# A decoder layer on one core: the first modulation and projection in quarters, with weights laid out in 4 KB pieces

## The chip, the cores and the metric

The kernel runs on one core of one Trainium2 chip. TensorE is called PE here (its weight loads PEld), VectorE DVE, ScalarE ACT, GpSimd POOL, and SyncE SP, which issues most DMAs. The metric is device time in microseconds (us) of one execution.

## The reference, cut to what matters

```python
mod = silu(c) @ w_ada + b_ada                  # (1, 6144); only the first 2048 columns matter here
shift1, scale1, ... = split(mod, 6)
h = rms_norm(x, norm1_g) * (1 + scale1) + shift1   # x: 1024 tokens x 1024
proj = h @ w_in                                # 1472 columns
q_lat, kv_lat, k_rope, x_lru, g_lru = split(proj)
# then attention on q_lat, kv_lat, k_rope; a gated linear recurrence on x_lru, g_lru;
# output projection, residual, and a routed expert FFN with the other four parts of mod
```

## The kernel before, in words

The tokens are taken in two halves of 512 (`n` or `hf` is 0 or 1). For each half, `stats(hf)` squares and sums the four 128-token tiles of x (`sq`, on ACT and DVE), takes the inverse root by a chain of small DVE operations (`rsq`, tiles `rs_x`, `rs_t`, result `iv8`) and scales the tiles in place. `turn(hf)` transposes them on PE into eight tiles `pt`, of which two PSUM banks hold two at a time. `modulate(hb)` computes half of shift1 and scale1: 32 products of a broadcast `silu(c)` with tiles `wada` into `pm`, then a copy `mrow0`, a turn into columns, and two small DVE operations that give `modc` and `sc1`. `lift(k)` applies them to the k-th slice (ACT, `xT`) and splits it into a rounded part `hTh` (a cast on DVE) and a rest `hTl` (a subtraction on DVE, for every fourth k on POOL).

The projection runs over twelve tiles of `w_in` (table `FT`: 0 `kl`, 1 `ql`, 2 `xl`, 3 `ql`, then three `xl`, `kr` and four `gl`). `load_in(i)` fetches tile i, `split_in(i)` splits it into `winh` (ACT) and `winl` (POOL for the first three, DVE after). `project(i, n)` is three matmuls of 128x512 for each of eight k, 24 in all, into a bank `pp`, of which there are three; `evac(i, n)` empties it: for tile 0 `latkh` (ACT), `latkl` (DVE) and squares `sqq`, for tile 1 `latq` and `sqq`, for an `xl` tile `xr` and `xc` (ACT), then three DVE operations for the convolution and a split `xch`, `xcl`. `sqq` goes to PE in matmuls `pc` with one column.

Before the change three tiles (K1 = 3) of half 0 are projected while `modulate(1)` is still being computed; `stats(1)` is written behind them, then the second half of the same three tiles, slice by slice with `turn(1)`; the other tiles follow, each with n = 0 and n = 1. From there on the recurrence's gates (`pg` matmuls, DVE chain from `lq` to a scan) are woven in, and the rest of the modulation (`wad`, `ada`). `rotary()` computes tables of sines and cosines on DVE and ACT (`rb`, `tab`); a short DVE chain (`ld`, `lp`) prepares the recurrence's constants. Each engine executes its list in order; the order comes from a scheduler that places the written instructions by its own estimates, except that SP keeps the written order through this stage (`pin`), and `issue_after` holds an instruction behind another. SP keeps up to eight transfers in flight.

Of the kernel before, what the change touches and what calls it, by code (L numbers as in the profile page):

```python
# [1774 lines left out]
```

## Time and profile before

| | |
|---|---|
| median of 3 runs | 814.96 us (814.83 to 815.29) |
| the profiled execution's own time | 816.14 us |
| its span (first to last instruction) | 814.4 us |
| PE busy in the span | 730.2 us (90%) |
| first matmul of the projection | 29.96 us after the span's start |
| three tiles, half 0 done | 56.6 us |
| three tiles, half 1 done | 78.9 us |

Read it like this: the profiled execution is one of its own, 1.2 us above the median, and 1.7 us of its time lie outside the span. The stage that the change touches ends at about 80 us; the other 730 us follow from it in order.

### The profile page before, as it was taken

To read this page: it belongs to the slowest core of one execution; us is meant where nothing else is said; L and a number is where in the kernel's file an instruction comes from. 1 tells how busy PE (TensorE), PEld (TensorE's weight loads), DVE (VectorE), ACT (ScalarE), POOL (GpSimd) and SP (SyncE) were. 2 spreads that over 40 slices of the span, in tenths; PEclk is the share of its full clock that TensorE was granted. 3 is DMA by queue.
4 is the path that set the end of the run, shared out by engine and by line. 5 is a ranking of instruction groups with operands and counts; after the bars stand their busy time and mean duration, and the time that the engine had idled before them with its cause. 6 is when DMAs were issued, how large, how long until landed. Compare 5 with 4: busy or idle time off the path is not lost. (4 is left out here: it accounts for less than half of the span.)

```text
span 814.4 us, 12262 instructions
## 1 busy us (share of the span) xinstructions
PE 730.2 (90%) x4257; PEld 470.3 (58%) x4257; DVE 447.6 (55%) x1334; ACT 317.3 (39%) x715; POOL 157.6 (19%) x150
## 2 busy tenths in 40 slices
PE   3799999989988989899999997699988789999994
PEld 1377776548876878788888886333233234333231
DVE  4597386869776468788884667434333122221311
ACT  3455456675344156667664444221201112120210
POOL 1121012102766102031311000212112111221101
PEclk9999999999999999999999998799989999999999
DMA  9952437682307403020154699899999999999993
GB/s 312 374 149 85 143 118 236 211 269 84 119 9 281 156 27 104 1 79 1 60 193 140 237 340 345 329 294 344 335 345 319 358 369 331 336 365 341 349 313 64
DMA packets 70976, 180.47 MB, mean 222 GB/s; under 512 B 8960, under 2 KB 22528, under 8 KB 70912
## 3 DMA queue, kind: packets, MB, share of 16 engines
q1 hardware_dynamic: 63328, 158.50, 54.9%
q0 software_dynamic: 7104, 21.00, 9.7%
q8 instruction: 34, 0.56, 0.3%
q10 hardware_dynamic: 480, 0.16, 0.1%
q14 instruction: 30, 0.25, 0.1%
HBM read 160.61 MB, written 22.95 MB: 225 GB/s over the span
## 5 line engine op out<-in xcount | busy, mean ns | idle before, releaser
L1649 PE MATMUL pgu<-ew,xeT 128*32 128x512 f32 (+1 forms) x928 | 166.4, 620 | 7.7 <-DMA ew<-in_w_e 7.5
L1649 PEld LDWEIGHTS pgu<-ew,xeT 128*32 128x32 f32 (+1 forms) x928 | 47.8, 122 | 100.2 <-issue 82.2
L1660 PE MATMUL py<-ew,hT 128*32 128x512 f32 (+1 forms) x464 | 78.5, 596 | 4.4 <-ACT hT L1634 4.4
L225 PE MATMUL pp<-hTh,winh 128*128 128x512 f32 x176 | 68.2, 400 | 5.8 <-DVE hTh L188 3.0
L226 PE MATMUL pp<-hTl,winh 128*128 128x512 f32 x176 | 70.1, 398 | 0.2 <-DVE hTl L469 0.2
L227 PE MATMUL pp<-hTh,winl 128*128 128x512 f32 x176 | 69.5, 396 | 0.0
L1663 DVE TENSOR_TENSOR y<-py,m_g 128x512 f32<-128x512 f32 (+1 forms) x40 | 27.6, 691 | 74.9 <-PE py L1660 70.0
L1623 ACT ACTIVATE sg<-pgu 128x256 f32<-128x256 f32 (+1 forms) x20 | 7.7, 386 | 130.4 <-PE pgu L1649 130.4
L1660 PEld LDWEIGHTS py<-ew,hT 128*32 128x32 f32 (+1 forms) x464 | 23.9, 120 | 49.8 <-issue 38.5
L1616 DVE TENSOR_SCALAR xeT<-pxe,gc,mc 128x128 f32<-128x128 f32 x80 | 27.4, 403 | 38.2 <-PE pxe L1610 38.2
L1634 ACT ACTIVATE hT<-pht 128x256 f32<-128x256 f32 (+1 forms) x20 | 7.6, 381 | 98.0 <-PE pht L1632 86.1
L1665 POOL DMA_INDIRECT out<-y,pki x13 | 20.7, 1594 | 115.4 <-DVE y L1663 91.3
L225 PEld LDWEIGHTS pp<-hTh,winh 128*128 128x128 f32 x176 | 33.4, 190 | 16.2 <-DVE hTh L188 4.0
L1625 DVE SCALAR_TENSOR_TENSOR hid<-sg,pkw,pgu 128x256 f32<-128x256 f32 (+1 forms) x13 | 6.2, 477 | 63.5 <-ACT sg L1623 63.5
L1614 ACT ACTIVATE xeT<-pxe,mc,gc 128x128 f32<-128x128 f32 x80 | 30.0, 461 | 25.9 <-PE pxe L1610 25.9
L226 PEld LDWEIGHTS pp<-hTl,winh 128*128 128x128 f32 x176 | 33.4, 190 | 9.9 <-issue 2.1
L227 PEld LDWEIGHTS pp<-hTh,winl 128*128 128x128 f32 x176 | 33.4, 190 | 8.3 <-DVE lq L587 0.8
L949 ACT ACTIVATE P<-pS,nb,scq 128x384 f32<-128x384 f32 (+2 forms) x48 | 32.3, 679 | 12.2 <-DVE nb L946 12.2
L983 PE MATMUL po<-PT,v 128*128 128x256 f32 (+1 forms) x160 | 35.8, 362 | 0.0
L1046 POOL TENSOR_TENSOR wo<-wo,m_g 128x256 f32<-128x256 f32 x32 | 28.2, 917 | 15.5 <-DMA wo<-in_w_out 15.5
L1610 PEld LDWEIGHTS pxe<-ident,xe 128*128 128x128 f32 x160 | 18.4, 145 | 21.0 <-issue 15.7
L983 PEld LDWEIGHTS po<-PT,v 128*128 128x128 f32 x160 | 28.8, 191 | 2.9
(424 smaller groups left out, 1615.0 us busy)
## 6 DMA issues: line engine op xcount, KB each, us to landing
ew<-in_w_e SPq DMA_DIRECT2D x186, 512.0 KB, 7.2
wad<-in_w_ada SPq DMA_DIRECT2D x64, 256.0 KB, 4.0
wada<-in_w_ada SPq DMA_DIRECT2D x16, 512.0 KB, 10.8
win<-in_w_in SPq DMA_DIRECT2D x12, 512.0 KB, 7.5
xt<-in_x SPq DMA_DIRECT2D x8, 512.0 KB, 6.6
wo<-in_w_out SPq DMA_DIRECT2D x8, 512.0 KB, 6.1
xr<-in_x SPq DMA_DIRECT2D x8, 512.0 KB, 4.6
x_d<-xr SPq DMA_DIRECT2D x8, 512.0 KB, 2.7
```

The costliest lines, as they stand in the source:

```text
L225: T.matmul(o, lhi, rhi, start=first, stop=False)
L226: T.matmul(o, lhi, rlo, start=False, stop=False)
L227: T.matmul(o, llo, rhi, start=False, stop=last)
L949: SC.activation(Pt[:, o:o + w], pss[ci], AF.Exp, scale=P["scq"][:, i:i + 1], bias=nb, accum_out=l[:, ci:ci + 1])
L983: T.matmul(po[:, o:], P["v"][:, js], PT[j // 4][:, j % 4, o:], start=(j == 0), stop=(j == nj - 1), skip_group_check=True)
L1046: EN[OPT["g1"]].tensor_mul(w[:, q:q + 256], w[:, q:q + 256], mrow["g1"][:, q:q + 256])
L1614: SC.activation(xT[a][:, c], pt[:, c], AF.Identity, scale=gc[:, k:k + 1], bias=sh2[:, k:k + 1])
L1616: last["dve"] = V.tensor_scalar(xT[a][:, c], pt[:, c], gc[:, k:k + 1], sh2[:, k:k + 1], op0=OP.mult, op1=OP.add).ins
L1649: T.matmul(pg[r], xT[k // 4][:, c + r.start:c + r.stop], w[k // 2][:, NS[k % 2]], start=(k == 0), stop=(k == 7), skip_group_check=True)
L1660: T.matmul(py[n][r], hT[:, a * 128 + r.start:a * 128 + r.stop], w[4 + a][:, NS[n]], start=(a == 0), stop=(a == 1), skip_group_check=True)
L1663: last["dve"] = V.tensor_mul(y[:rows, NS[n]], py[n][:rows], mrow["g2"][:rows, NS[n]]).ins
L1665: G.indirect_dma_start(out=out, out_offset=bass.IndirectOffsetOnAxis(ap=idx, axis=0), in_=y[r0:r0 + idx.shape[0]], in_offset=None, compute ...
```

## The change

`modulate` is called for quarters (two slices k each, 32 products of 128 columns) in place of halves (four slices, 256 columns); its copy `mrow0` moves from ACT to DVE. The loads of `w_in` tiles 0 to 2 stand between those of the modulation's quarters, then tile 3, the second half of x and tile 4. After each quarter its two slices are lifted, the next `w_in` tile is split, and the tiles that are there advance by these slices. Tile 3 is projected for n = 0 behind `stats(1)`, so that its second visit does n = 1 alone. Every `winl` and `hTl` is now computed on DVE. `rotary()` no longer starts at the head and is drained later; the chain `ld`, `lp` is held behind the scaling of the last x tile. On the host, `w_in` is laid out as one contiguous 4 KB row for each partition and tile (before: eight pieces of 512 B), and the first 2048 columns of `w_ada` as rows of 4 KB (before: pieces of 2 KB).

```diff
@@ -114,7 +114,7 @@
...
-... "lo": "VVVG", ... "in_l1": "G", ...
+... "lo": "VVVV", ... "in_l1": "V", ...
@@ -247,12 +247,9 @@
         kind, j = FT[i]
-        M = 64 if kind == "kr" else 128
-        f0 = FCOL[kind] + j * 128
-        w = blk("win")
-        v = t3(w, 8)[:, :, :M]
-        SY.dma_start(v, A["w_in"][:, f0:f0 + M].rearrange("(k p) f -> p k f", p=128))
-        wraw[i] = v
+        w = blk("win")[:, :512 if kind == "kr" else 1024]
+        SY.dma_start(w, A["w_in"][i * 128:(i + 1) * 128, :w.shape[1]])
+        wraw[i] = t3(w, 8)
 
@@ -279,22 +276,22 @@
     load_x(0)
-    for i in range(OPT["lw"]):
-        load_in(i)
     wada = {}
 
-    def load_ada(hb):
-        for k in range(8):
-            w = wada[hb, k] = blk("wada")
-            SY.dma_start(t3(w, 2), A["w_ada"][k * 128:(k + 1) * 128, :2048].rearrange(
-                "p (s h d) -> p s h d", s=2, h=2)[:, :, hb])
-
-    load_ada(0)
-    for i in range(OPT["lw"], OPT["lw2"]):
-        load_in(i)
-    load_ada(1)
-    for i in range(OPT["lw2"], OPT["lw4"]):
-        load_in(i)
+    def load_ada(q):
+        for k in range(4):
+            w = blk("wada")
+            r = (q * 4 + k) * 128
+            SY.dma_start(w, A["w_ad0"][r:r + 128, :])
+            wada[q, 2 * k], wada[q, 2 * k + 1] = w[:, :512], w[:, 512:]
+
+    for q in range(4):
+        if q < 3:
+            load_in(q)
+        load_ada(q)
+    load_in(3)
+    load_x(1)
+    load_in(4)
     row = const.tile([128, NROW], F32, name="row")
@@ -365,7 +362,7 @@
             if OPT["xsc"][t] == "V":
-                V.tensor_scalar(xs[t], xs[t], iv8[:, t:t + 1], None, op0=OP.mult)
+                last["xsc"] = V.tensor_scalar(xs[t], xs[t], iv8[:, t:t + 1], None, op0=OP.mult).ins
             else:
@@ -382,8 +379,7 @@
     stats(0)
-    for i in range(OPT["lw"]):
-        split_in(i)
+    split_in(0)
     drain(turn(0))
@@ -437,26 +433,21 @@
 
-    def modulate(hb):
-        pm = bank("pm")[:, :256]
+    def modulate(q):
+        pm = bank("pm")[:, :128]
         for k in range(8):
-            yield
             for i in range(4):
-                T.matmul(pm[32 * i:32 * i + 32], cs32[:, k, :], wada[hb, k][:, i * 256:i * 256 + 256],
+                T.matmul(pm[32 * i:32 * i + 32], cs32[:, k, :], wada[q, k][:, i * 128:i * 128 + 128],
                          start=(k == 0), stop=(k == 7), skip_group_check=True)
-        mrow0 = half("mrow0")[:, :256]
-        SC.activation(mrow0, pm, AF.Copy)
+        mrow0 = half("mrow0")[:, :128]
+        V.tensor_copy(mrow0, pm)
         pm2 = bank("pm2")
-        for c in range(2):
-            T.matmul(pm2[:, c:8:2], mrow0[:, c * 128:(c + 1) * 128], ident[:, 0:128:32], start=True, stop=True)
-        hs = slice(hb * 4, hb * 4 + 4)
-        V.tensor_add(t3(modc, 2)[:, :, hs], t3(pm2[:, :8], 2), t3(C("bada"), 2)[:, :, hs])
-        V.scalar_tensor_tensor(sc1[:, hs], modc[:, 8 + hb * 4:12 + hb * 4], 1.0, C("n1g")[:, hs], op0=OP.add, op1=OP.mult)
+        T.matmul(pm2[:, :4], mrow0, ident[:, 0:128:32], start=True, stop=True)
+        hs = slice(q * 2, q * 2 + 2)
+        V.tensor_add(t3(modc, 2)[:, :, hs], t3(pm2[:, :4], 2), t3(C("bada"), 2)[:, :, hs])
+        V.scalar_tensor_tensor(sc1[:, hs], modc[:, 8 + q * 2:10 + q * 2], 1.0, C("n1g")[:, hs], op0=OP.add, op1=OP.mult)
 
     rot = rotary()
-    if OPT["ro"] == 0:
-        next(rot)
-    drain(modulate(0))
     sh1 = modc[:, 0:8]
@@ -467,14 +458,6 @@
         EN[OPT["lo"][k % 4]].tensor_sub(hTl[k][:, ns], xT[k], hTh[k][:, ns])
-
-    for k in range(4):
-        lift(k, xT[k], 0)
-    for i in range(OPT["lw4"], OPT["lw3"]):
-        load_in(i)
-    load_x(1)
-    for i in range(OPT["lw3"], OPT["k1"]):
-        load_in(i)
 
@@ -677,26 +660,21 @@
     K1 = OPT["k1"]
-    mod = modulate(1)
-    split_in(1)
-    if OPT["ro"] == 1:
-        next(rot)
-    for i in range(K1):
-        for k in range(4):
-            drain(project(i, 0, range(k, k + 1)))
-            if i < 2:
-                next(mod)
-        if i == 1:
-            drain(mod)
-            for k in range(4, 8):
-                lift(k, xT[k], 0)
-            for j in range(2, K1):
-                split_in(j)
-    for i in range(K1):
-        if i == OPT["st"]:
-            stats(1)
-        drain(project(i, 0, range(4, 8)))
-        evac(i, 0)
+    begun = [0] * K1
+    for q in range(4):
+        modulate(q)
+        for k in (2 * q, 2 * q + 1):
+            lift(k, xT[k], 0)
+        if q < 3:
+            split_in(q + 1)
+        for i in range(min(q + 2, K1)):
+            drain(project(i, 0, range(begun[i], 2 * q + 2)))
+            begun[i] = 2 * q + 2
+            if q == 3:
+                evac(i, 0)
+    stats(1)
+    drain(project(K1, 0))
+    evac(K1, 0)
     tn = turn(1)
@@ -709,29 +687,27 @@
     with tc.issue_after(last["sq"]):
         SC.activation(le, lx, AF.Exp, scale=-1.0)
-    V.tensor_scalar(ld, le, 2.0, None, op0=OP.add)
...
+    with tc.issue_after(last["xsc"]):
+        V.tensor_scalar(ld, le, 2.0, None, op0=OP.add)
...
     pin.close()
-    drain(rot)
...
-    load_in(K1)
-    load_in(K1 + 1)
@@ -741,11 +717,11 @@
             load_gate(j)
-        for n in range(2) if i >= K1 else (1,):
+        for n in range(2) if i > K1 else (1,):
             for _ in project(i, n) if i >= K1 else ():
...
                     next(ag, None)
-            if n == (0 if i >= K1 else 1):
+            if n == (0 if i > K1 else 1):
                 gates()
@@ -756,8 +732,9 @@
             wsp.pop(i)
+        if i == 2:
+            drain(rot)
         if i == 1:
-            split_in(K1)
             V.tensor_scalar(rst, rsti, 0, None, op0=OP.is_equal)
@@ -1737,6 +1714,12 @@
         f["w_down"].reshape(NE, 2, 128, D).transpose(0, 2, 1, 3).reshape(NE, 128, 2048)], axis=2).reshape(NE * 128, 6144)
+    win = np.zeros((len(FT), 128, 1024), np.float32)
+    for i, (kind, j) in enumerate(FT):
+        m = 64 if kind == "kr" else 128
+        f0 = FCOL[kind] + j * 128
+        win[i, :, :8 * m] = f["w_in"][:, f0:f0 + m].reshape(8, 128, m).transpose(1, 0, 2).reshape(128, 8 * m)
+    win = win.reshape(len(FT) * 128, 1024)
     wr = np.concatenate([f["w_router_group"], f["w_router_expert"]], axis=1)
@@ -1750,8 +1733,9 @@
     return {
+        "w_ad0": np.ascontiguousarray(f["w_ada"][:, :2048].reshape(4, 2, 128, 2, 4, 256).transpose(4, 0, 2, 1, 3, 5)).reshape(2048, 1024),
         "x": f["x"], "pos_c": f["positions"].reshape(NT, 128).T, "pos_r": f["positions"], "cols": cols, "rows": rows,
-        "w_ada": f["w_ada"], "b_ada": f["b_ada"], "w_in": f["w_in"], "w_q_b": f["w_q_b"], "w_kv_b": f["w_kv_b"],
+        "w_ada": f["w_ada"], "b_ada": f["b_ada"], "w_in": win, "w_q_b": f["w_q_b"], "w_kv_b": f["w_kv_b"],
         "lru_wa": f["lru_wa"], "lru_wx": f["lru_wx"], "w_out": f["w_out"], "norm2_g": f["norm2_g"],
```

What stands where, engine by engine, follows. First PE around the first modulation's end, before: `pm_313` and `pm_423` are the turns of the two halves (L451), `pm<-wada` the modulation's products, `pp` the projection.

```order
L451 MATMUL pm_313<-ident,mrow_311 128x4 x2
L445 MATMUL pm<-wada,cs_157 32x256 x12
L225 MATMUL pp<-hTh,winh 128x512
L445 MATMUL pm<-wada,cs_157 32x256 x4
L226 MATMUL pp<-hTl,winh 128x512
L227 MATMUL pp<-hTh,winl 128x512
```

And now, where `pm_318` and `pm_385` are the turns of the first two quarters:

```order
L445 MATMUL pm_318<-ident,mrow_316 128x4
L440 MATMUL pm<-wada,cs_169 32x128 x32
L225 MATMUL pp<-hTh,winh 128x512
L226 MATMUL pp<-hTl,winh 128x512
L227 MATMUL pp<-hTh,winl 128x512
L225 MATMUL pp<-hTh,winh 128x512
L445 MATMUL pm_385<-ident,mrow_383 128x4
L440 MATMUL pm<-wada,cs_169 32x128 x8
```

The projection now starts behind the first quarter's turn and the second quarter's products, and the third quarter's products stand between its matmuls. Second, ACT between the last lift of half 0 and the first lift of half 1, before (`xT_257` is that last lift, `sq` are the squares of `stats(1)`, `pp_362`, `pp_388` and `pp_452` the banks of tiles 0 to 2):

```order
L467 ACTIVATE xT_257<-xT_257,modc_259,sc1_260 128x512
L361 ACTIVATE sq_465,ssx_160<-xt_338 128x512
L361 ACTIVATE sq_467,ssx_160<-xt_338 128x512
L361 ACTIVATE sq_469,ssx_160<-xt_340 128x512
L361 ACTIVATE sq_471,ssx_160<-xt_340 128x512
L711 ACT_TABLE_LOAD
L711 ACTIVATE le_720<-lx_719 128x4
L276 ACTIVATE winh_448<-win_346 128x1024
L221 ACTIVATE latkh_514<-pp_362,col_75 128x512
L613 ACTIVATE latq_538<-pp_388,col_75 128x512
```

And now (`pp_336`, `pp_343`, `pp_415` are the banks of tiles 0 to 2):

```order
L458 ACTIVATE xT_269<-xT_269,modc_271,sc1_272 128x512
L221 ACTIVATE latkh_554<-pp_336,col_75 128x512
L596 ACTIVATE latq_572<-pp_343,col_75 128x512
L535 ACTIVATE xr_588<-pp_415 128x512
L536 ACTIVATE xc_589<-pp_415,col_75 128x512
L585 ACTIVATE sqq_558<-pp_336 128x512
L585 ACTIVATE sqq_574<-pp_343 128x512
L358 ACTIVATE sq_599,ssx_172<-xt_125 128x512
L358 ACTIVATE sq_601,ssx_172<-xt_125 128x512
L358 ACTIVATE sq_603,ssx_172<-xt_127 128x512
L358 ACTIVATE sq_605,ssx_172<-xt_127 128x512
L689 ACT_TABLE_LOAD
```

The squares of the second half have moved from before the banks' emptying to behind it. Third, DVE at the same place as it stands now (before, the squares came directly behind the last cast, and `latkl` and the convolution `xc` behind the scaling of x):

```order
L460 TENSOR_TENSOR hTl_544<-xT_269,hTh_543 128x512
L222 SCALAR_TENSOR_TENSOR latkl_555<-pp_336,col_75,latkh_554 128x512
L360 SCALAR_TENSOR_TENSOR sq_607,ssx_172<-xt_129 128x512
L360 SCALAR_TENSOR_TENSOR sq_609,ssx_172<-xt_129 128x512
L360 SCALAR_TENSOR_TENSOR sq_611,ssx_172<-xt_131 128x512
L360 SCALAR_TENSOR_TENSOR sq_613,ssx_172<-xt_131 128x512
L539 SCALAR_TENSOR_TENSOR xc_589<-xr_588,col_75,xc_589 128x511
L539 SCALAR_TENSOR_TENSOR xc_589<-xr_588,col_75,xc_589 128x510
L361 TENSOR_TENSOR ss8_171<-ssx_172 128x4
L539 SCALAR_TENSOR_TENSOR xc_589<-xr_588,col_75,xc_589 128x509
```

Behind these rows follow the first four operations of `rsq`, then `xcl_591` (which needs ACT's `xch_590`, behind `le`), and then the rest of `rsq`. `latkl` and the convolution now stand ahead of the statistics' end.

## Rows read from the trace of the kernel before

**Rows 1.** From the page: the span of the profiled execution and its instructions.

```profile
span 814.4 us, 12262 instructions
```

**Rows 2.** Busy time by stretch, within the first 180 us: start and end, length, then busy us (and number) of PE, PEld, DVE, ACT and POOL, granted clock of TensorE, mean share of the DMA engines, GB/s.

```profile
28.60:41.20 12.60, 8.75 (x66) 3.78 (x58) 5.57 (x10) 6.86 (x10) 3.64 (x2) 1.00 1.07 368
41.20:56.60 15.40, 15.14 (x58) 12.09 (x59) 15.29 (x52) 6.69 (x15) 3.99 (x2) 0.89 0.64 184
56.60:78.90 22.30, 22.11 (x121) 18.54 (x119) 14.91 (x32) 12.98 (x19) 3.90 (x2) 1.00 0.26 78
...
100.00:120.00 20.00, 19.25 (x100) 14.28 (x98) 17.62 (x26) 11.70 (x17) 2.38 (x1) 1.00 0.31 96
```

**Rows 3.** Timeline of PE, start, length, line, operation and its tiles, count, in brackets the idle time before it and what ended it.

```profile
25.25 0.66 PE L376 MATMUL pt<-ident,xt 128*128 128x128 f32 x4
...
27.41 1.50 PE L445 MATMUL pm<-wada,cs 128*32 128x256 f32 x24
...
29.96 0.51 PE L225 MATMUL pp<-hTh,winh 128*128 128x512 f32 x1 [1.04 <-DVE hTh L188]
...
37.56 0.61 PE L451 MATMUL pm<-ident,mrow 128*128 128x4 f32 x4 [0.50 <-ACT mrow L448]
...
46.63 0.39 PE L225 MATMUL pp<-hTh,winh 128*128 128x512 f32 x1
46.85 0.39 PE L226 MATMUL pp<-hTl,winh 128*128 128x512 f32 x1
...
56.60 1.03 PE L376 MATMUL pt<-ident,xt 128*128 128x128 f32 x8
57.48 1.84 PE L605 MATMUL pc<-ones_f,sqq 128*128 128x1 f32 x16
...
59.99 0.96 PE L225 MATMUL pp<-hTh,winh 128*128 128x512 f32 x3
...
80.47 0.50 PE L225 MATMUL pp<-hTh,winh 128*128 128x512 f32 x1 [1.60 <-ACT xc L553]
```

**Rows 4.** Timeline of ACT, read in the same way.

```profile
14.40 2.19 ACT L370 ACTIVATE xt<-xt,iv 128x1024 f32<-128x1024 f32 x2 [5.71 <-DVE iv L213]
...
28.63 2.93 ACT L467 ACTIVATE xT<-xT,modc,sc 128x512 f32<-128x512 f32 x4 [1.51 <-DVE sc L454]
...
43.28 0.61 ACT L361 ACTIVATE sq<-xt 128x512 f32<-128x512 f32 x1
...
44.00 1.28 ACT L711 ACT_TABLE_LOAD   x1
45.30 0.21 ACT L711 ACTIVATE le<-lx 128x4 f32<-128x4 f32 x1
...
50.91 0.69 ACT L221 ACTIVATE latkh<-pp,col 128x512 fp32r<-128x512 f32 x1 [4.15 <-PE pp L227]
...
56.51 1.08 ACT L602 ACTIVATE sqq<-pp 128x512 f32<-128x512 f32 x2 [4.34 <-DVE latkl L222]
57.48 0.60 ACT L552 ACTIVATE xr<-pp 128x512 f32<-128x512 f32 x1
57.96 0.79 ACT L553 ACTIVATE xc<-pp,col 128x512 f32<-128x512 f32 x1
```

**Rows 5.** Timeline of DVE, with the POOL row that runs beside the second stretch of it.

```profile
29.48 0.43 DVE L188 CAST hTh<-xT 128x512 fp32r<-128x512 f32 x1 [0.88 <-ACT xT L467]
29.93 0.69 DVE L469 TENSOR_TENSOR hTl<-xT,hTh 128x512 fp32r<-128x512 f32 x1
...
38.53 2.36 POOL L277 TENSOR_TENSOR winl<-win,winh 128x1024 fp32r<-128x1024 f32 x1 [4.08 <-ACT winh L276]
...
39.45 1.73 DVE L188 CAST hTh<-xT 128x512 fp32r<-128x512 f32 x1 [0.88 <-ACT xT L467]
...
46.87 2.90 DVE L363 SCALAR_TENSOR_TENSOR sq<-xt 128x512 f32<-128x512 f32 x1
...
49.70 0.68 DVE L363 SCALAR_TENSOR_TENSOR sq<-xt 128x512 f32<-128x512 f32 x1
...
50.62 0.17 DVE L199 TENSOR_SCALAR rs_x<-ss 128x4 f32<-128x4 f32 x1
...
53.01 2.74 DVE L368 TENSOR_SCALAR xt<-xt,iv 128x1024 f32<-128x1024 f32 x4
...
100.73 1.23 DVE L277 TENSOR_TENSOR winl<-win,winh 128x1024 fp32r<-128x1024 f32 x1 [0.30 <-ACT winh L276]
...
130.12 1.23 DVE L583 SCALAR_TENSOR_TENSOR lq<-lq,rcap 128x1024 f32<-128x1024 f32 x1 [6.38 <-ACT lq L578]
```

**Rows 6.** Busy time by stretch again, in shorter stretches, for the transfer rate and the granted clock (columns as in rows 2).

```profile
32.00:36.00 4.00, 4.00 (x27) 1.59 (x25) 1.06 (x3) 0.00 (x0) 1.28 (x1) 1.00 1.13 319
38.00:42.00 4.00, 1.44 (x6) 0.61 (x5) 2.84 (x5) 3.85 (x7) 2.36 (x1) 1.00 1.03 397
42.90:46.30 3.40, 3.40 (x10) 2.69 (x9) 3.37 (x7) 3.18 (x7) 1.60 (x1) 0.54 1.10 336
```

**Rows 7.** From the page: the issues of the first modulation's loads, KB each and the median time to their landing; and from the timeline of SP's queue when they are issued (start, length from the first to the last).

```profile
wada<-in_w_ada SPq DMA_DIRECT2D x16, 512.0 KB, 10.8
4.97 18.60 SPq L289 DMA_DIRECT2D wada<-in_w_ada  x16
```

**Rows 8.** Waits of PE in the stretch from 56 to 330 us: who waited for whom, us in total, times, the longest wait.

```profile
PE pm L494 <- DMA wad<-in_w_ada: 3.2, 2, 1.7
```

More of the change, by code (lines that the diff above doesn't have):

```diff
@@ L116 @@
     "P": "VVVVVVVV", "ssh": 1, "ssk": 0, "in_lo": "V", "xc_lo": "V", "lk_lo": "V", "wk_lo": "G", "ii": "G", "g1": "G", "h2": "G", "hi": "VV",
-    "pt": "VS", "gl0": 6, "xa": 3, "pf": {31: 4, 32: 3, 22: 1, 25: 1, 28: 3, 7: 2, 11: 4, 12: 8, 16: 1, 17: 30}, "sqA": "G", "mg": 61, "h2p": "SSSSSSSS", "xp": "SSSSVVVV", "rh": "G", "hk": 7, "sep": 0, "rw": 2, "glw": 54, "mL": "V", "k1": 3, "gs": 1, "adv": 1, "adv0": 0, "fly": 4, "fly0": 4, "lo": "VVVG", "ptc": "SSV", "lw": 1, "lw2": 1, "lw3": 2, "lw4": 3, "ro": 0, "in_l1": "G", "xsc": "VSVSVVVV", "pin": "Y", "st": 0, "ta": 2, "sq": "SSVVSSVV", "sqL": "G",
+    "pt": "VS", "gl0": 6, "xa": 3, "pf": {31: 4, 32: 3, 22: 1, 25: 1, 28: 3, 7: 2, 11: 4, 12: 8, 16: 1, 17: 30}, "sqA": "G", "mg": 61, "h2p": "SSSSSSSS", "xp": "SSSSVVVV", "rh": "G", "hk": 7, "sep": 0, "rw": 2, "glw": 54, "mL": "V", "k1": 3, "gs": 1, "adv": 1, "adv0": 0, "fly": 4, "fly0": 4, "lo": "VVVV", "ptc": "SSV", "lw": 1, "lw2": 1, "lw3": 2, "lw4": 3, "ro": 0, "in_l1": "V", "xsc": "VSVSVVVV", "pin": "Y", "st": 0, "ta": 2, "sq": "SSVVSSVV", "sqL": "G",
 }
@@ L711, in layer @@
         SC.activation(le, lx, AF.Exp, scale=-1.0)
-    V.tensor_scalar(ld, le, 2.0, None, op0=OP.add)
-    V.reciprocal(ld, ld)
-    V.tensor_mul(ld, le, ld)
-    V.tensor_mul(l2, ld, ld)
-    V.tensor_scalar(lp, l2, 1.0 / 15, 1.0 / 13, op0=OP.mult, op1=OP.add)
-    for m in (11, 9, 7, 5, 3, 1):
-        V.tensor_mul(lp, lp, l2)
-        V.tensor_scalar(lp, lp, 1.0 / m, None, op0=OP.add)
-    V.tensor_mul(lp, lp, ld)
-    V.tensor_scalar(lx, C("lam"), -1.0, 0.0, op0=OP.mult, op1=OP.max)
-    V.scalar_tensor_tensor(lp, lp, 2.0, lx, op0=OP.mult, op1=OP.add)
-    V.tensor_scalar(sp4, lp, 4.0, None, op0=OP.mult)
-    sp8 = const.tile([128, 4], F32, name="sp8")
-    V.tensor_scalar(sp8, lp, -8.0, None, op0=OP.mult)
+    with tc.issue_after(last["xsc"]):
+        V.tensor_scalar(ld, le, 2.0, None, op0=OP.add)
+        V.reciprocal(ld, ld)
+        V.tensor_mul(ld, le, ld)
+        V.tensor_mul(l2, ld, ld)
+        V.tensor_scalar(lp, l2, 1.0 / 15, 1.0 / 13, op0=OP.mult, op1=OP.add)
+        for m in (11, 9, 7, 5, 3, 1):
+            V.tensor_mul(lp, lp, l2)
+            V.tensor_scalar(lp, lp, 1.0 / m, None, op0=OP.add)
+        V.tensor_mul(lp, lp, ld)
+        V.tensor_scalar(lx, C("lam"), -1.0, 0.0, op0=OP.mult, op1=OP.max)
+        V.scalar_tensor_tensor(lp, lp, 2.0, lx, op0=OP.mult, op1=OP.add)
+        V.tensor_scalar(sp4, lp, 4.0, None, op0=OP.mult)
+        sp8 = const.tile([128, 4], F32, name="sp8")
+        V.tensor_scalar(sp8, lp, -8.0, None, op0=OP.mult)
     pin.close()
-    drain(rot)
     rst = big.tile([128, 1024], BF, name="rst", tag="h", bufs=NHALF)
```

## The prediction

> **What bounds the kernel now.** I read the page first: a span of 814.4 us [rows 1], of which PE is busy for nine tenths. So what counts is where PE waits and what it is given to do, and I went on to the busy times by stretch. From 56.6 to 78.9 us PE works 22.11 of 22.3 us, and from 41.2 to 56.6 us 15.14 of 15.4, there at a mean clock of 0.89. Between 28.6 and 41.2 us it is busy for only 8.75 of 12.6, and from 100 to 120 us for 19.25 of 20, beside a DVE at 17.62 [rows 2]. The stage of the change therefore has a poor head, and behind it PE is the bound. The timeline says why: PE's first projection matmul comes at 29.96 us, when the whole first half of the modulation is turned and lifted; the second half's turn at 37.56 waits for ACT's copy [rows 3]. Two smaller things: PE waits 1.60 us for a bank before 80.47 [rows 3], and two waits for `wad`, 3.2 us in all, lie further on [rows 8]. The profiled execution's own time is 816.14 us, 1.2 above the median; the sum below is a difference inside that execution, and I take the same difference off the median.
>
> **The head, up to the end of half 0.** Statistics and scaling of the first half don't change: the last scaling ends at 14.40 + 2.19 = 16.6 us [rows 4]. Behind it come eight transposed tiles, each emptied from one of two banks by a copy of 128x512. I price that at 0.69 us, a DVE operation of this size [rows 5], which gives 16.6 + 8 x 0.69 = 22.1 and about 22.5 with the last turn; before, PE's last `pt` lies at 25.25, woven between the products of a half [rows 3]. Then the first quarter's copy, turn and two small operations on DVE, at 0.2 us each (a small one takes 0.17 [rows 5]): the first lift at 23.3, before 28.63 [rows 4]. Lift, cast and split take 29.96 - 28.63 = 1.3 us up to the first matmul: 24.6 instead of 29.96.
>
> The next quarters' products are written between the matmuls. Before, 24 instructions of 256 columns took 1.50 us [rows 3], or (1.50 - 0.38)/23 = 49 ns each. A quarter has 32 products of 128 columns, each two instructions on PE, 64 in all. If the time goes by columns this is 1.6 us a quarter; if each instruction costs the same, 3.1. I take 1.75, near the lower end, since at 49 ns for 256 columns PE seems to stream them and not to pay a fixed price. From the second quarter on PE has enough to do: 36 matmuls at 0.227 (46.85 - 46.63 is 0.22 [rows 3]) are 8.2 us, with the third quarter's products 9.9, so from about 25.4 to 35.3, where the third turn stands. Its lift is 0.75 later at 36.05, the fourth's about 4.85 later at 40.9 (18 matmuls of 0.227, the turn and the small operations), and the last `hTl` comes 3.0 us behind that, at 43.9 (two lifts, two casts of 0.43 and two splits of 0.69 in turn). The last matmuls of the three tiles end at about 46.3, before 56.6.
>
> **The loads.** The last issue before is at 4.97 + 18.60 = 23.6 us, and a median landing takes 10.8 [rows 7]: 34.4. Now two more tiles of 0.52 MB stand ahead of the last piece, 2.6 us more: 37.0. In 4 KB pieces the stream ran at 397 GB/s (x, 38 to 42 us), in 512 B pieces at 319 (`win`, 32 to 36 us) [rows 6], so the three `win` tiles gain 0.3 us each and the last piece lands at 35.7 to 37.0. The fourth quarter's products are needed at about 36 to 38, so I cost the loads at nothing; their cover is the 36 matmuls, and if it is gone each microsecond late counts once. The Trainium skill, *DMA: Bandwidth & Descriptors*, section Specifications, says that transfers of 512 B and more reach line rate. This speaks against the layout; the row of 319 against 397 disagrees with it here. By the rule the layout would gain nothing and the loads would run 1 us late: the sum would be -3.0 in place of -4.0.
>
> **The second half's statistics.** ACT first empties banks: `latkh` 45.6 to 46.3, `latq`, `xr`, `xc` to 48.1, two `sqq` to 49.1 (0.6 to 0.8 each [rows 4]); then four squares of 0.61 to 51.5, the table load 1.28, `le` 0.21, and `xch` at 53.1 to 53.7. DVE is free from 43.9 and waits for `latkh`; `latkl` to 47.1, four squares of 0.68 to 50.1, two operations of the convolution to 51.5, the sum of the statistics at 51.65, the last convolution step to 52.5, four small ones, `xcl` behind `xch` to 54.4, the rest of `rsq` with some rows of the rotary to 56.7. Four scalings of 2.74 in all [rows 5] end at 59.4; before they end at 53.01 + 2.74 = 55.75. So x is ready 3.65 us **later** although half 0 is ready 10 us earlier: the emptying now stands ahead of it in both queues. POOL's work goes to DVE: a `winl` of 1.23 and an `hTl` of 0.69. Against this stands that casts beside POOL's 2.36 us took 1.73 instead of 0.43, and squares 2.90 instead of 0.68 [rows 5]; I take the pair as even.
>
> Meanwhile PE has tile 3's n = 0. It waits some 2 us for a bank, then 24 matmuls, 5.45 us, to about 55.5; both lie beside the statistics and cost nothing as long as x isn't ready before 57. Behind the scaling: transposes done 59.7, first lift 60.5 at its end, then `ld`, `lp` (about a dozen small operations before the first cast, 2.3 us with what lies between) to 61.75, first matmul of half 1 at 62.2 against 59.99 [rows 3], +2.2. From there the same work as before, with some 0.2 us more of waits at its end for the rotary's rows that now stand in these queues: half 1 of the three tiles ends at 81.3 against 80.47 - 1.60 = 78.87 [rows 3]: **+2.4**.
>
> **The sum.** Behind it tile 3 has n = 1 alone: minus 24 x 0.227 = **-5.45**, and minus its group of `pc`, half of the 1.84 us for two groups [rows 3], **-0.92**. Together +2.4 - 5.45 - 0.92 = -4.0 us: 812.1 in the profiled execution, 811.0 in the median. This gain passes on if PE stays the bound; in the rest nothing changes but the start.
>
> **Rivals.** *The quarter's products cost by instruction*: 3.1 us instead of 1.75 for each. Two quarters stand where PE is busy ahead of the last lift, so half 0 and the statistics behind it come 2.5 us later, and the time is 813.5. For it: the 49 ns are measured at 256 columns alone.
>
> *The clock falls*: between 56 and 62 us PE has little more than transposes. Before, 38 to 42 us shows PE busy 1.44 of 4 us, and right behind, at 42.9 to 46.3, the granted clock is 0.54 with PE busy all through [rows 6], the lower of the two levels (1.2 GHz). 3.4 us at 0.54 hold 1.8 us of work, so 1.6 are lost: 812.7. Against it: the old loss at the same place goes, since PE now has the fourth quarter's work there. The Trainium skill, *TensorE: Matmul & The Clock Gate*, section on how HAM oscillation bites in real kernels, states that idle gaps bring the clock down again; these rows agree.
>
> *Nothing arrives behind the stage*: the `wad` transfers run at their own pace, so that PE, 4 us earlier, waits 4 us longer for them, beside the 3.2 us it waits now [rows 8]; or the first quarter isn't earlier, because DVE, which now has copy, small operations, splits and `winl`, holds its chain up, and the 4 us are lost in the head. 815.0.
>
> *The statistics aren't late*: ACT's and DVE's queues run closer than I laid them and x is scaled by 57. Then the +2.4 falls away: 808.6.
>
> *Slower: the recurrence and not PE sets the pace behind half 1.* The convolution of tile 2's second half comes 2.4 us later, and with it the gates' chain on DVE and ACT. DVE is busy 17.62 of 20 us there [rows 2], but idles 6.38 us before `lq` at 130.12 [rows 5]. PE comes 4.0 us earlier and the chain 2.4 later, 6.4 in all: as much as that idle time. If part of the idle time is needed, the gates end last, tile 3's work saved on PE shows up as waiting, and the +2.4 is passed on: 817.4. It decides from the point where DVE has no idle time left before that `lq`. Against it: PE at 19.25 of 20 in the same stretch.
>
> **How the numbers follow.** Forecast 0.46, with its own range of 809 to 813 (half 0's end 1 us either way, the bounds of the small operations); products by instruction 0.13; the clock 0.10; nothing arrives 0.09; statistics not late 0.10; slower 0.12. This measurement can tell about 0.2%, 1.6 us, from no change. Faster by more (under 813.3): the forecast, the clock, the better case and part of the products, 0.70. Same: nothing arrives and the rest of the products, 0.17. Slower: 0.13. The range reaches from below the better case, 807.0, to 815.5, which takes in all cases but the slower one and little at the low end.
>
> **What would show it.** First projection matmul near 24.6; 64 product instructions of a quarter in 1.75 us; three tiles' half 0 done near 46; tile 3's n = 0 between 48 and 56; last scaling of x at 59.4, after a DVE that waits for ACT's `xch`; first half-1 matmul near 62; PE's next bank wait at 81. No POOL work before 80. The prediction is wrong if the head's stretch shows PE waiting for DVE at each quarter, if the granted clock is low after 60, if the waits for `wad` grow beyond 3.2, or if DVE has no idle time left before the second gate's `lq`.

## The result, and the profile after

The changed kernel takes 824.14 us (median of four, 823.37 to 825.29) against 814.89 us in the same comparison: 1.0103 times the time, with an interval of 1.0075 to 1.0131. The forecast was 811.0, and the range ended at 815.5. The profiled execution took 823.37 us, with this span and this busy time of PE:

```profile
span 821.6 us, 12524 instructions
PE 734.6 (89%) x4385; PEld 479.9 (58%) x4385; DVE 455.2 (55%) x1349; ACT 317.7 (39%) x713; POOL 145.2 (18%) x143
```

Busy time by stretch after the change, with the columns of [rows 2]:

```profile
28.60:41.20 12.60, 12.60 (x150) 9.41 (x151) 6.07 (x13) 4.50 (x6) 0.00 (x0) 1.00 1.03 407
41.20:49.60 8.40, 8.13 (x36) 5.99 (x34) 4.58 (x11) 2.55 (x5) 0.00 (x0) 1.00 0.40 144
49.60:56.00 6.40, 4.79 (x23) 3.96 (x22) 5.76 (x17) 6.37 (x15) 0.00 (x0) 1.00 0.00 0
...
60.00:68.50 8.50, 7.62 (x34) 6.33 (x35) 8.50 (x30) 3.80 (x6) 0.00 (x0) 0.61 0.05 15
68.50:85.20 16.70, 16.68 (x79) 13.45 (x77) 11.21 (x37) 6.41 (x9) 0.00 (x0) 0.99 0.31 95
```

The head has become full: PE is busy for all of 28.6 to 41.2 us, where it worked 8.75 of 12.6 before [rows 2]. What comes behind is new: between 49.6 and 60.1 us PE waits twice, 1.61 and 1.26 us, and then it runs at a mean granted clock of 0.61. PE's timeline, read as in [rows 3]:

```profile
24.30 1.95 PE L440 MATMUL pm<-wada,cs 128*32 128x128 f32 x64
26.18 0.50 PE L225 MATMUL pp<-hTh,winh 128*128 128x512 f32 x1
...
38.22 0.28 PE L445 MATMUL pm<-ident,mrow 128*128 128x4 f32 x2
...
49.25 0.39 PE L227 MATMUL pp<-hTh,winl 128*128 128x512 f32 x1
51.24 0.50 PE L225 MATMUL pp<-hTh,winh 128*128 128x512 f32 x1 [1.61 <-ACT xc L536]
...
60.06 1.05 PE L588 MATMUL pc<-ones_f,sqq 128*128 128x1 f32 x8 [1.26 <-ACT sqq L585]
...
64.96 1.63 PE L225 MATMUL pp<-hTh,winh 128*128 128x512 f32 x3
...
86.79 0.50 PE L225 MATMUL pp<-hTh,winh 128*128 128x512 f32 x1 [1.61 <-ACT xc L536]
```

The first projection matmul stands at 26.18 instead of 29.96, the three tiles' half 0 ends at 49.6 instead of 56.6, and then the lead is gone: the first matmul of half 1 comes at 64.96 (before 59.99), and half 1 ends at 86.79 - 1.61 = 85.2 instead of 78.9 [rows 3], **6.3 us later**. Tile 3's n = 0 is done by then, which before was 6.4 us of work still to do (24 matmuls and a group of `pc`, by the prediction's prices). So at this point the two kernels are level, and the loss of 7 to 9 us (7.2 in the profiled executions, 9.25 in the medians) arises behind it.

I follow it by a landmark that every kernel here has: the first score matmul of the attention (`pS`), at 287.58 us before and at 294.33 after, 6.75 later. From there to the routed experts both run alike (the first expert matmul is 6.77 later). In the experts' part one execution differs from another by some us with nothing changed there: from its first to its last matmul 286.8 us in the profile of before and 282.0 in one of the experiments (e_lift_first). So the landmarks tell more than totals.

### The profile page after: what moved, and what is told of

The parts are those of the page before. It is cut to its first block, busy times and chain, and to the rows that moved or that the text cites. A ratio compares the mean times of both kernels' runs of the same rounds, so it can differ in the third digit from the quotient of the medians.

```text
span 821.6 us, 12524 instructions
## 1 busy us (share of the span) xinstructions
PE 734.6 (89%) x4385; PEld 479.9 (58%) x4385; DVE 455.2 (55%) x1349; ACT 317.7 (39%) x713; POOL 145.2 (18%) x143
## 5 line engine op out<-in xcount | busy, mean ns | idle before, releaser
L1626 PE MATMUL pgu<-ew,xeT 128*32 128x512 f32 (+1 forms) x928 | 163.3, 603 | 9.6 <-DMA ew<-in_w_e 9.6
L1637 PE MATMUL py<-ew,hT 128*32 128x512 f32 (+1 forms) x464 | 81.3, 628 | 2.7 <-ACT hT L1611 2.7
L1637 PEld LDWEIGHTS py<-ew,hT 128*32 128x32 f32 (+1 forms) x464 | 24.6, 125 | 51.2 <-issue 43.8
L572 POOL TENSOR_TENSOR gt_wx<-gt_wx,xc 128x1024 f32<-128x1024 f32 x4 | 10.5, 2618 | 164.1 <-ACT gt_wx L554 144.7
```

Source lines behind the costliest of these rows:

```text
L1626: T.matmul(pg[r], xT[k // 4][:, c + r.start:c + r.stop], w[k // 2][:, NS[k % 2]], start=(k == 0), stop=(k == 7), skip_group_check=True)
L1637: T.matmul(py[n][r], hT[:, a * 128 + r.start:a * 128 + r.stop], w[4 + a][:, NS[n]], start=(a == 0), stop=(a == 1), skip_group_check=True)
```

## The experiments

All ratios are against the kernel before on the same chip, where its median was between 814.9 and 816.5; so compare ratios, not medians, from row to row. "Half 1 ends" and the rest are from each kernel's single profiled execution, in us from its span's start. They scatter: `after` and `e_wad_pace` have the same instructions in the same order on every engine up to half 1's end, and it stands at 85.2 in one and 86.9 in the other (from 60 to 64 us the granted clock was 0.73 in the one and 0.53 in the other). A difference of less than 2 us in these columns is not shown by itself.

| kernel | half 1 ends | last `wad` product ends | attention starts | median | ratio to before (interval) |
|---|---|---|---|---|---|
| before | 78.9 | 178.5 | 287.6 | 814.9 | 1 |
| after | 85.2 | 188.9 | 294.3 | 824.1 | 1.010 (1.007 to 1.013) |
| e_stats_first | 84.8 | 188.4 | 293.9 | 821.1 | 1.008 (1.005 to 1.010) |
| e_pool_back | 89.2 | 192.5 | 298.4 | 827.3 | 1.016 (1.012 to 1.019) |
| e_before_4k | 78.5 | 177.5 | 286.7 | 814.9 | 0.999 (0.996 to 1.002) |
| e_tile3_late | 86.1 | 184.9 | 293.3 | 821.2 | 1.006 (1.004 to 1.008) |
| e_both | 79.6 | 179.7 | 289.5 | 814.7 | 0.997 (0.993 to 1.000) |
| e_both_rot | 80.7 | 179.8 | 289.9 | 816.7 | 0.999 (0.996 to 1.002) |
| e_wad_pace | 86.9 | 177.8 | 287.2 | 813.8 | 0.998 (0.995 to 1.002) |
| e_wad_stats | 85.1 | 176.0 | 285.5 | 812.7 | 0.995 (0.993 to 0.998) |
| e_lift_first | 81.8 | 173.9 | 283.3 | 808.7 | 0.991 (0.988 to 0.994) |
| e_before_wadlate | 78.8 | 184.8 | 291.2 | 817.7 | 1.004 (1.000 to 1.007) |

In the short diffs below + and - are against the kernel that the expectation names.

**e_before_4k.** 

> The kernel before with the 4 KB layouts of w_in and w_ada alone, halves as they were. The layout as a price by itself: if nothing waits for these loads, 814.5 to 815.5; if the last piece of the modulation is waited for, its 1 to 1.5 us come off: 813.5. A time above 817 would mean that the layout costs something behind the head.

```diff
...
-        SY.dma_start(v, A["w_in"][:, f0:f0 + M].rearrange("(k p) f -> p k f", p=128))
...
+        SY.dma_start(w, A["w_in"][i * 128:(i + 1) * 128, :w.shape[1]])
...
+            SY.dma_start(w, A["w_adh"][(hb * 8 + k) * 128:(hb * 8 + k + 1) * 128, :])
...
```

No difference within the interval: the layout by itself neither gains nor costs time in the kernel before.

**e_pool_back.** 

> The changed kernel with every fourth hTl and the winl of the first three tiles on POOL again. Theory A: DVE's extra work of some 5 us isn't on the path, and POOL's running beside DVE stretches DVE's casts as before: 824 to 826. Rival: DVE's queue is what makes the quarters and the last lifts late, and the time falls by 1 to 2: 822 to 823.

```diff
-... "lo": "VVVV", ... "in_l1": "V", ...
+... "lo": "VVVG", ... "in_l1": "G", ...
```

Worse by 4.0 us, at half 1's end and at the attention alike, where the prediction had called the pair even. (It priced one `winl` and one `hTl`; before the change POOL has three and two of them up to half 0's end.) The scheduler also placed the fourth quarter's products elsewhere (in four groups instead of one), so the 4.0 are not split between POOL's work and the order.

**e_stats_first.** 

> The changed kernel with one thing undone: stats(1) is written before the three tiles' banks of half 0 are emptied, not behind it. Theory A (the head and the late statistics cost the time): ACT stood idle 45.4 to 48.8 and DVE 47.0 to 49.5 in the changed kernel, the squares fit there, x is scaled by about 55 instead of 61.9, half 1 of the three tiles ends some 3 to 6 us sooner than 85.2, and the time is 818 to 821. Theory B (the loss arises behind half 1, in the stage of the gates, whatever the head does): the half 1 ends sooner but the time stays at 823 to 825.

```diff
             if q == 3:
+                if i == 0:
+                    stats(1)
                 evac(i, 0)
-    stats(1)
```

The statistics came sooner, as expected, and half 1 hardly did (84.8), which neither theory said. The ratio of 1.008 isn't told apart from the 1.010 of the changed kernel. First DVE, then ACT in this kernel, from 51 us on:

```profile
51.10 2.74 DVE L365 TENSOR_SCALAR xt<-xt,iv 128x1024 f32<-128x1024 f32 x4
```

```profile
57.03 0.63 ACT L218 ACTIVATE xch<-xc 128x512 fp32r<-128x512 f32 x1 [1.26 <-DVE lp L696]
61.65 0.69 ACT L596 ACTIVATE latq<-pp,col 128x512 f32<-128x512 f32 x1 [3.99 <-PE pp L227]
62.23 0.59 ACT L585 ACTIVATE sqq<-pp 128x512 f32<-128x512 f32 x1
62.71 1.45 ACT L458 ACTIVATE xT<-pt,modc,sc 128x512 f32<-128x512 f32 x2
```

x is scaled by 53.8 instead of 61.9 and its first slices are turned at 54.3, but the first lift stands at 62.71: in ACT's queue it is behind `latq` and `sqq` of tile 3, and ACT waits 3.99 us for PE to finish that tile. So tile 3's n = 0 lay "beside the statistics" only as long as the statistics were late. The edit has a price too: the squares now stand ahead of the last casts on DVE, and half 0 ends at 51.7 instead of 49.6.

**e_tile3_late.** 

> The changed kernel with tile 3's n = 0 back behind half 1 of the three tiles. Theory B (work on PE behind half 1 is hidden by the gates' chain, so the change gained nothing by taking it away there; beside the late statistics it was hidden too): 822 to 825, and half 1 ends near 85 as it did. Theory A (PE is the bound behind half 1): the 6.4 us come back on top: 830.

```diff
-    drain(project(K1, 0))
-    evac(K1, 0)
...
-        for n in range(2) if i > K1 else (1,):
+        for n in range(2) if i >= K1 else (1,):
...
-            if n == (0 if i > K1 else 1):
+            if n == (0 if i >= K1 else 1):
```

**e_both** (this and e_stats_first together). 

> The changed kernel with both undone: stats(1) ahead of the banks' emptying, and tile 3's n = 0 behind half 1. With the statistics first alone, x was scaled at 53.8 but ACT's first lift stood behind tile 3's emptying and came at 62.7. Theory B (tile 3 was moved from a place where it is hidden to one where it is not): the lift comes at about 55, half 1 ends at 76 to 77 against 78.9 of the kernel before, and the time is 811 to 813. Theory A (PE is the bound behind half 1): half 1 as early, but 6.4 us more work behind it against the changed kernel, so that it stays near the kernel before or above: 815 to 819.

**e_both_rot.** 

> As the one with both undone, and the first part of the rotary's rows (some 4 us of DVE) written into DVE's idle time at 33 to 38 us instead of beside half 1's lifts. If the rows between the casts delay half 1, its end comes 0.5 to 1.5 sooner than without: 810 to 812. If PE paces half 1 they cost nothing: no difference beyond 0.5.

```diff
+        if q == 1:
+            next(rot)
...
```

Tile 3 put back alone: half 1's end and the attention's start move by 0.9 and 1.0 us, in opposite directions and within the scatter, and the time, 821.2, is near theory B's figure. But this edit also gives `wad` its two steps back, which I had not seen when I wrote the expectation; the runs below price the two, by way of e_wad_pace, at -7.1 and +6.1, so that theory B's figure came out of two effects that nearly cancel. With the statistics first as well (e_both), half 1 ends at 79.6, where I had expected 76 to 77, and the time is not told apart from that of before. The rotary's rows moved into DVE's idle time (e_both_rot) brought nothing.

**e_before_short3** (18 matmuls of the kernel before are left out; the routing of the tokens then differs, so only the part up to the attention is read). 

> The kernel before, with 18 of the 24 matmuls of tile 3's n = 0 left out (slices k = 0 and 3 alone), nothing else moved: 18 x 0.227 = 4.1 us less work on PE behind half 1, at the place where the change saves 5.45 and 0.92. Theory A (PE is the bound there): 814.9 - 4.1 = 810.8. Theory B (the gates' chain on ACT, DVE and POOL and its waits set the pace, so work saved on PE turns into waiting): 814 to 816.

```diff
...
                 yield
+                if (i, n) == (K1, 0):
+                    yield
...
-            for _ in project(i, n) if i >= K1 else ():
+            for _ in project(i, n, (0, 3) if (i, n) == (K1, 0) else range(8)) if i >= K1 else ():
```

The second `yield` keeps the number of `wad` steps at tile 3. The attention starts at 289.2, 1.6 *later*, with 4.1 us less work. Three of PE's idle times in it:

```profile
102.71 0.80 PE L225 MATMUL pp<-hTh,winh 128*128 128x512 f32 x1 [2.92 <-ACT xc L555]
...
153.17 1.06 PE L494 MATMUL pm<-wad,cs 128*32 128x512 f32 x8 [1.35 <-DMA wad<-in_w_ada]
...
167.50 1.93 PE L494 MATMUL pm<-wad,cs 128*32 128x512 f32 x8 [2.01 <-DMA wad<-in_w_ada]
```

A wait of 2.92 for a bank stands where PE waited 0.75 for `sqq` before, and the waits for `wad` go on (4.0 us in all, 3.2 before). This looked like theory B, that the gates set the pace and PE's saving is worth nothing. The next runs show that theory to be wrong as a general rule. Where the saving went can be read from the busy times between half 1's end and the attention, first the kernel before, then this one (columns as in [rows 2]):

```profile
78.87:287.58 208.71, 193.93 (x953) 146.32 (x953) 144.50 (x252) 106.80 (x169) 59.19 (x57) 0.99 0.48 159
78.60:289.20 210.60, 193.76 (x935) 145.41 (x935) 144.23 (x252) 107.03 (x169) 59.62 (x57) 0.97 0.47 157
```

With 18 matmuls fewer PE is busy for the same time, 193.8 us against 193.9, at a mean granted clock of 0.97 instead of 0.99, and it idles 2.1 us longer. So the work that was saved reappears in PE's own busy time, at the lower clock, and what makes the attention later is further waiting.

**e_wad_pace.** 

> The changed kernel, with the rest of the modulation (wad) advanced two steps at each half of tile 3's visit instead of one, so that wad's products keep the place they had before (in the changed kernel the last ones come at 188.9 instead of 178.5). Theory B (the gates' chain): no change, 823 to 825. Rival C (the waits of 3.6, 2.4 and 3.7 us and the low clock behind 150 us come from wad's late products): they go, 819 to 821.

```diff
-                for _ in range(OPT["adv"]):
+                for _ in range(2 if i == K1 else OPT["adv"]):
                     next(ag, None)
```

Theory B said 823 to 825, the rival 819 to 821; measured were 813.8, below both and not told apart from the kernel before, although half 1 ends even 1.7 us later than in the changed kernel. This one line is worth 7.1 us at the attention's start. Where they arise is read from the two kernels side by side. In it `pmc` is the turn of the `wad` products into columns, `pk` a turn of `krT` (the `kr` tile), `kb` ACT's squares of `pk`, `gelu` the emptying of a `gl` tile's bank, and `sqL` sums of squares for a later norm. First PE in the changed kernel, behind 186 us:

```profile
187.86 1.07 PE L477 MATMUL pm<-wad,cs 128*32 128x512 f32 x8
...
193.48 0.95 PE L492 MATMUL pmc<-ident,adab 128*128 128x4 f32 x8
194.29 1.98 PE L625 MATMUL pk<-ident,krT 128*128 128x64 f32 x16
...
198.87 0.80 PE L225 MATMUL pp<-hTh,winh 128*128 128x512 f32 x1 [2.42 <-ACT gelu L637]
```

and ACT beside it:

```profile
184.53 1.06 ACT L571 ACTIVATE gt_wa<-gt_wa 128x1024 f32<-128x1024 f32 x1
196.31 0.60 ACT L629 ACTIVATE kb<-pk 128x512 f32<-128x512 f32 x1 [10.72 <-PE pk L625]
...
198.22 1.57 ACT L637 ACTIVATE gelu<-pp 128x512 f32<-128x512 f32 x3
```

The same place in e_wad_pace, PE's `pk` and then ACT:

```profile
188.59 1.89 PE L625 MATMUL pk<-ident,krT 128*128 128x64 f32 x16
```

```profile
185.99 1.06 ACT L571 ACTIVATE gt_wa<-gt_wa 128x1024 f32<-128x1024 f32 x1
190.51 0.60 ACT L629 ACTIVATE kb<-pk 128x512 f32<-128x512 f32 x1 [3.46 <-PE pk L625]
...
192.43 1.09 ACT L637 ACTIVATE gelu<-pp 128x512 f32<-128x512 f32 x2
```

ACT is in step until 185 or 186. Then it waits for PE's `pk`: 10.72 us in the changed kernel, 3.46 with `wad` at its old pace. On PE `pk` stands behind the late `wad` products and their turn `pmc`, at 194.29 instead of 188.59. Behind `kb` on ACT wait the `gelu`s that empty the banks, and so PE itself, 2.42 us. Further losses follow: a wait of 3.7 us for POOL's `sqL` before 240.19, 3.6 for a bank before 157 (1.6 with the old pace), and a low clock behind such waits:

```profile
230.00:240.00 10.00, 5.21 (x31) 4.53 (x30) 6.03 (x12) 5.00 (x14) 10.00 (x10) 0.97 0.04 16
240.00:250.00 10.00, 9.81 (x34) 8.62 (x35) 9.05 (x43) 4.15 (x18) 2.35 (x4) 0.52 0.01 2
```

(PE busy 5.21 of 10 us, and in the next 10 us a clock of 0.52; before, those stretches granted 0.83 and 1.00.) Waits and clock can be told apart by PE's busy time from half 1's end to the attention, first the changed kernel, then e_wad_pace:

```profile
85.19:294.33 209.14, 192.59 (x921) 145.11 (x921) 149.71 (x251) 105.92 (x167) 60.52 (x57) 0.96 0.47 158
86.90:287.20 200.30, 188.49 (x922) 142.09 (x921) 143.96 (x251) 105.61 (x167) 59.91 (x57) 0.98 0.48 165
```

The work is the same. The stretch is 8.8 us longer in the changed kernel: 4.1 us of it PE is busy longer, at a mean clock of 0.96 instead of 0.98, and 4.7 us it idles longer. So about half of the price is the clock.

Why does the change move `wad`? The loop over the tiles advances the generator of the modulation's rest once at each half of a `project`. Tile 3's n = 0 was taken out of this loop, and its two steps with it, so that every later step of `wad` comes two half tiles later.

**e_before_wadlate.** 

> The kernel before with one thing changed: wad isn't advanced at tile 3's n = 0, so that its steps come two half tiles later, as they do in the changed kernel. If wad's late products are what loses PE's saved time: last wad at about 188 instead of 178.5, the attention starts 5 to 8 us later, 820 to 823. If they cost only together with the late half 1: 814 to 816.

```diff
-                for _ in range(OPT["adv"]):
+                for _ in range(0 if (i, n) == (K1, 0) else OPT["adv"]):
```

The cause put into the kernel before by itself. Its attention starts 3.6 us later, and PE shows two of the same idle times (and one of 2.58 for a bank before 104.14, which the changed kernel hasn't):

```profile
195.87 0.80 PE L225 MATMUL pp<-hTh,winh 128*128 128x512 f32 x1 [2.60 <-ACT gelu L654]
...
237.97 1.05 PE L1059 MATMUL pc<-ones_f,sqL 128*128 128x1 f32 x8 [3.30 <-POOL sqL L660]
```

```profile
78.80:291.20 212.40, 198.00 (x953) 150.15 (x953) 146.80 (x252) 107.23 (x169) 59.13 (x57) 0.96 0.48 157
```

That is half of what the old pace gives back in the changed kernel, between the two figures that I had given. Against the row of the kernel before (under e_before_short3) PE is busy 4.1 us longer for the same work, at a mean clock of 0.96 instead of 0.99, and idles no longer, 14.4 us against 14.8: the new waits stand there in place of the two for `wad`, 3.2 us [rows 8], which are gone here. In the changed kernel and in e_wad_pace PE nowhere waits for `wad`'s loads, so that nothing offsets the new waits there. In the median only 0.4% is left of the loss, with an interval that nearly touches none.

**e_wad_stats.** 

> The same without moving the lifts: wad at its old pace and stats(1) first. With the statistics first alone half 1 ended at 84.8 (85.2 without), so a gain of 0 to 2 against wad's old pace alone: 812 to 814. If the order of stats(1) still matters by itself: 809 to 811.

**e_lift_first.** 

> The changed kernel with three things: wad kept at its old pace (two steps at each half of tile 3's visit), stats(1) ahead of the banks' emptying, and the first two slices of half 1 transposed and lifted ahead of tile 3's n = 0, so that ACT's lifts stand before tile 3's emptying and PE works on tile 3 while they run. If tile 3's early place is the rest of the loss: first half-1 matmul at about 60, half 1 ends at 79 as in the kernel before, with tile 3's 6.4 us behind it: last projection at about 217, 808 to 810. If the stage behind half 1 has no slack for that (as with tile 3 shortened in the kernel before): last projection at 221 to 224, 813 to 816.

Beside the lines of e_wad_pace and e_stats_first, which e_wad_stats has together, its edit is this (`turn(1)` contains the lifts):

```diff
...
+    tn = turn(1)
+    for _ in range(OPT["ta"]):
+        next(tn)
     drain(project(K1, 0))
     evac(K1, 0)
-    tn = turn(1)
-    for k in range(-OPT["ta"], 8):
+    for k in range(8):
...
```

e_wad_stats came out as expected, 812.7. At the attention's start the statistics first are now worth 1.7 us, and the lifts ahead of tile 3's emptying another 2.2. Neither is clear of the scatter by itself; the two together are, 3.9 us, and the intervals of e_wad_pace and e_lift_first don't overlap. ACT and PE in e_lift_first:

```profile
55.77 1.46 ACT L458 ACTIVATE xT<-pt,modc,sc 128x512 f32<-128x512 f32 x2
57.45 0.64 ACT L218 ACTIVATE xch<-xc 128x512 fp32r<-128x512 f32 x1 [0.23 <-ACT xT L458]
61.76 0.69 ACT L596 ACTIVATE latq<-pp,col 128x512 f32<-128x512 f32 x1 [3.67 <-PE pp L227]
```

```profile
59.54 1.84 PE L588 MATMUL pc<-ones_f,sqq 128*128 128x1 f32 x16
...
61.56 0.60 PE L373 MATMUL pt<-ident,xt 128*128 128x128 f32 x4
61.92 0.48 PE L225 MATMUL pp<-hTh,winh 128*128 128x512 f32 x1
...
283.30 0.38 PE L912 MATMUL pS<-kTh,qTh 128*128 128x256 f32 x1 [0.84 <-DVE xr L1062]
```

The lifts run at 55.77 while PE works on tile 3, half 1 starts at 61.92 without a gap, and the clock from 60 to 68 us is 1.00. Half 1 ends 2.95 us later than before (I had expected level, with its first matmul at 60), tile 3's 6.4 us are off the list, and the attention starts 4.3 us sooner. The time is 808.7 against 816.3: 0.991 (0.988 to 0.994), faster than the kernel before and than the changed one, and inside the expected 808 to 810. Only 4.3 us of the gain lie ahead of the attention; the rest stands in the experts' part, where nothing was changed, and isn't explained.

## Why the prediction was wrong, point by point

**The step that failed most: "in the rest nothing changes but the start".** The sum had no term for `wad`. Its steps are counted by the very loop from which tile 3's n = 0 was taken; this stands in the code, but the prediction followed only what stands near the change. Measured: 7.1 us at the attention's start (294.3 to 287.2), which is the whole of the loss there (6.75). Forecast and measurement lie 10.8 us apart at this place (-4.0 against +6.75): this step is 7.1 of it, half 1's end, next, 3.9. About half of it is waiting and half PE's lower clock. That the delay costs something by itself is shown by e_before_wadlate (3.6). There the clock's part is as large, 4.1 us of busy time, and the new waits are offset by the 3.2 us of waits for `wad`'s loads that go; this is read from the profiles and was not tried by a run of its own. None of the four signs by which the prediction was to be known as wrong could catch the delay: one of them, the low clock after 60, came; PE hardly waits for DVE in the head, the waits for `wad` fell to nothing, and DVE has idle time left before that `lq`.

**Half 1's end: +2.4 predicted, +6.3 measured.** Three terms were too small.
- The head. First projection matmul 26.18 against my 24.6, third quarter's turn 38.22 against 35.3, half 0's end 49.6 against 46.3. Of this 1.6 us is the start: the first lift came at 24.80, which I had at 23.3, since the copies that empty the transposes took until 24.07 and not 22.1.

```profile
23.47 0.60 ACT L186 ACTIVATE xT<-pt 128x512 f32<-128x512 f32 x1 [0.84 <-PE pt L373]
24.80 1.52 ACT L458 ACTIVATE xT<-xT,modc,sc 128x512 f32<-128x512 f32 x2 [0.73 <-DVE sc L448]
```

From the first projection matmul to half 0's end it took 23.4 us instead of 21.7, and PE was busy for nearly all of it (12.60 of 12.60 us, then 8.13 of 8.40), so most of this is work and not waiting: a quarter's products took 1.95 us instead of 1.75 in one piece, and the third quarter's, in four pieces between the projection's matmuls, 0.64 to 0.65 for each. The price by instruction (3.1 us) is ruled out.
- The statistics then kept the lag: the last scaling of x ended at 61.9, I had 59.4, and the first matmul of half 1 came 2.8 later than forecast. The chain that the prediction wrote down (emptying, squares, table load, `xch`, `xcl`, rest of `rsq`) is the one in the trace. DVE's part of it:

```profile
49.49 0.75 DVE L222 SCALAR_TENSOR_TENSOR latkl<-pp,col,latkh 128x512 fp32r<-128x512 f32 x1 [2.54 <-ACT latkh L221]
...
56.68 0.69 DVE L219 TENSOR_TENSOR xcl<-xc,xch 128x512 fp32r<-128x512 f32 x1 [0.53 <-ACT xch L218]
...
59.20 2.73 DVE L365 TENSOR_SCALAR xt<-xt,iv 128x1024 f32<-128x1024 f32 x4
```

- The clock, a rival that I gave 0.10, came on top:

```profile
60.00:64.00 4.00, 3.12 (x19) 2.49 (x20) 4.00 (x16) 1.46 (x3) 0.00 (x0) 0.73 0.00 0
64.00:68.00 4.00, 4.00 (x16) 3.51 (x15) 4.00 (x13) 2.01 (x3) 0.00 (x0) 0.50 0.12 33
```

At 64 to 68 us the granted clock is 0.50, the level of 1.2 GHz, with half 1's first matmuls in it; 20.2 us from the first to the last matmul of half 1 instead of the 19.1 that I had. The rule that the prediction cited from the Trainium skill (*TensorE: Matmul & The Clock Gate*, section on how HAM oscillation bites in real kernels), that idle gaps bring the clock down, agrees: here it fell behind gaps of 1.61 and 1.26 us. The stretches at 60 to 68 and 240 to 250 us and the one of [rows 6] show it.

**"Both lie beside the statistics and cost nothing"** was half right. In the changed kernel it held, because the statistics were as late; but tile 3's n = 0 lay at 51 to 59 us and not at 48 to 56. e_stats_first shows that tile 3's emptying stands ahead of the lifts in ACT's queue, and e_lift_first that this is worth some 2 us once the rest is in order.

**What was right.** The saving itself: with all of `wad`'s steps in the loop in both, tile 3's early n = 0 moves the attention from 293.3 (e_tile3_late) to 287.2 (e_wad_pace), 6.1 us, where I had 5.45 + 0.92 = 6.37. Loads at nothing (e_before_4k). The Trainium skill's page *DMA: Bandwidth & Descriptors*, section Specifications, gives 512 B as the least transfer for line rate. It is contradicted by the rate and not by the time: the loads ran at 407 GB/s from 28.6 to 41.2 us, against 319 in a stretch of mostly 512 B pieces [rows 6], and e_before_4k shows no gain by it. With the three repairs the kernel does about what the sum said of the change: half 1 ends 2.95 later (+2.4 in the sum), and the attention starts 4.3 sooner (4.0). That the first of these agrees is chance: the sum has half 0 end at 46.3 and x scaled at 59.4, and in e_lift_first it is 51.8 and 54.0.

**The rivals.** *Nothing arrives behind the stage* is refuted in both its forms: PE has no wait for `wad`'s loads in the changed kernel, and the first quarter was earlier (26.18 against 29.96). *The statistics aren't late*: they were later still, 61.9.

**The slower rival** had the right sign and the wrong mechanism. It decided "from the point where DVE has no idle time left before that `lq`"; in the changed kernel 2.61 us of idle time were left there:

```profile
133.07 1.23 DVE L566 SCALAR_TENSOR_TENSOR lq<-lq,rcap 128x1024 f32<-128x1024 f32 x1 [2.61 <-ACT lq L561]
```

And e_wad_pace ends half 1 8 us later than the kernel before and still starts the attention on time, because PE's saving does pass on. In e_before_short3 it did not: the profile shows it lost to the clock and to waits. What set these off stays open; the loads of tiles 3 and 4 also stand elsewhere in SP's queue there than in the changed kernel, and this was not tried apart.

## What to carry to other kernels

When a piece of work is taken out of a loop, look for everything that this loop counts or paces: here a generator was advanced once per half tile, and two lost steps cost 7.1 us, more than the 6.1 to 6.4 us that moving the tile could gain. Read busy time beside idle time: the same work at a lower clock is a loss that no wait shows. Work moved to an earlier "free" place is free only if its emptying doesn't stand ahead of the next stage in another engine's queue; ask of each queue, not of PE alone. And follow a change by landmarks in the trace up to where both kernels run alike; the total mixes in parts that vary by themselves.
